# Last quarter of a second feed-forward product: two corrections on VectorE instead of accumulating DMA, and another place for the end of two row tiles

## The chip, the cores and the metric

The kernel runs on one core of a Trainium2 chip. A core has TensorE (PE, matrix products into PSUM), VectorE (DVE), ScalarE (ACT) and GpSimd (POOL), which run their own instruction streams and meet at semaphores, and SyncE (SP), which here only issues transfers. Transfers are issued from the SP, ACT and POOL queues and carried by 16 DMA engines. A transfer issued from POOL can add to what stands at its destination; the text calls that a *send*.

The metric is device time in microseconds (us) of one execution; each figure for a kernel is the median of its runs.

## The reference, cut to what matters

One encoder layer on 512 rows of width 1024. Attention branches give `h`; the part that matters here is the feed-forward block and the last norm, with `D_FF` = 4096:

```python
u2 = rmsnorm(h, g_ffn[l])
h = h + jnp.square(jax.nn.relu(u2 @ w_ff1[l])) @ w_ff2[l]
...
return rmsnorm(h, g_final)
```

`rmsnorm(h, g)` is `h * rsqrt(mean(h * h) + 1e-6) * g` by row.

## The kernel before

`h` lives in SBUF as four row tiles `hN[0..3]` of 128 x 1024 in float32 (the order listings call them `h_3650` to `h_3653`, the profile `h`). Every float32 product is made from two parts of each factor, a rounded `hi` (a cast on ACT, L203) and a remainder `lo` (a subtraction on DVE, L204), in three matmuls (`mm3`, L151 to L153: hi times hi, lo times hi, hi times lo). A weight therefore has to be loaded, cast and split before PE can use it.

The feed-forward block is done in four quarters of `D_FF` (`q` = 0 to 3). Within a quarter each of the two products is a 2 x 2 block product made of seven half-size products instead of eight, by Strassen's scheme in Winograd's form. The text calls the seven products of the second one P1 to P7. Their order is

```python
ORDER = (1, 2, 5, 6, 3, 7, 4)
```

`second_product(q)` runs over that list. For each product `n` it takes two weight chunks (`factor`, i = 0, 1), and for each of two row tiles `t` of 128 rows it accumulates 2 x 2 x 3 matmuls of 128 x 512, 24 in a product. Then `evac(q, n, t, ps)` adds the result to the quarter blocks of `h`: `C(i, j, t)` is column half `j` of row tile `2 * i + t`. So row tiles 0 and 1 are the upper row blocks, 2 and 3 the lower. Weights of P5, P6, P7 and P4 are sums of two chunks and are made by a send into the buffers `b11`, `b12` (`b` in the profile).

P1 and P5 stay in PSUM over all four quarters (`held`). P6 and P7 of the first three quarters are summed in `R6`, `R7`. In the last quarter (`last`) the pieces are put together:

- P1, P2: a copy from PSUM to a scratch tile `sq` on ACT, and a send of it into `C(0, 0, t)`. P1 also gives `R6[t] = P1 - R6[t]`.
- P6: E = `R6[t]` - P6, G = P5 - E (in `s1[t]`, the listing's `s_4588`, `s_4589`), both on DVE; then sends of E into `C(1, 0, t)` and of G into `C(1, 1, t)` and `C(0, 1, t)`.
- P3: a copy and a send into `C(0, 1, t)`.
- P7: two DVE adds into `C(1, 1, t)` and `C(1, 0, t)`.
- P4: a DVE add into `C(1, 0, t)`.

`C(0, 0, t)` is complete after P2, `C(0, 1, t)` after P6 and P3, `C(1, 1, t)` after P7 and `C(1, 0, t)` after P4.

`finish(t, c, n)` is the last norm of row tile `t`, in two calls. Each squares and sums column half `c` (`sumsq`, ACT, L805; with `n` = 0 a one-column step on DVE, L807, follows). With `n` = 0, or if `t < 2`, it multiplies the half by the gain `gl` (L1036), on POOL for row tiles 0 and 1 and on DVE for 2 and 3. With `n` = 1 it makes r (`ms` on DVE, L812; a power on POOL, L813), multiplies both halves by r (ACT, L1041, or r and gain in one DVE instruction, L1043) and writes them out (L1044), one from ACT's queue and one from SP's.

PE's order is that of the code. On the other engines a scheduler with its own model of time decides where an instruction stands in the stream, and each engine then takes its stream strictly in that order.

Of the kernel before, what the change touches and what calls it, by code (L numbers as in the profile page):

```python
# [14 lines left out]
ALU = mybir.AluOpType  # L15
# [46 lines left out]
def hybrid_block(ctx, tc, chunks, wst, xT, memT, xN, cols, gffn, gfin, wup, cst, out):  # L62
    nc = tc.nc
# [5 lines left out]
    def nm(s):  # L69
        uid[0] += 1  # L70
        return f"{s}_{uid[0]}"
# [13 lines left out]
    def at_(shape=None):  # L85
        return pa.tile(shape or [P, 512], F32, tag="a", name=nm("a"))
# [68 lines left out]
    def gT(key, rhi, rlo, evac, n=S):  # L155

        hi, lo = (t.rearrange("p (k c) -> p k c", k=KT) for t in (get_w(key) if isinstance(key[0], str) else key))
        ps = mmt()
        for k in range(KT):
            mm3(ps[:, :n], hi[:, k, :], lo[:, k, :], rhi[:, k, :], rlo[:, k, :], k == 0, k == KT - 1)  # L160
            if k == KT - 1:
                evac(ps)
            yield

    def gN(keys, lhs, nt, mk, evac, tail=1, get=None):


        pss = [mk() for _ in range(nt)]
        n = len(keys)
        steps = [[j] for j in range(n - tail)] + [list(range(n - tail, n))]  # L170
        for js in steps:
            ws = {j: [t.rearrange("p (k c) -> p k c", k=2) for t in (get or get_w)(keys[j])] for j in js}
            for t in range(nt):
                for j in js:
                    for kk in range(2):
                        k = 2 * j + kk
                        a, b = lhs(k, slice(t * P, (t + 1) * P))
                        mm3(pss[t], a, b, ws[j][0][:, kk, :], ws[j][1][:, kk, :], k == 0, k == 2 * n - 1)
                        if k == 2 * n - 1:
                            evac(t, pss[t])  # L180
                        yield
# [85 lines left out]
    with pool("front") as fp:  # L267
# [24 lines left out]
        ps = at_()  # L292
# [510 lines left out]
    def sumsq(sq, src, t, c, n):  # L803

        nc.scalar.activation(sq, src[:, 512 * c:512 * c + 512], AF.Square, accum_out=hss[:, t, n:n + 1])  # L805
        if n == 0:
            nc.vector.tensor_scalar(hss[:, t, 0:1], hss[:, t, 0:1], 1.0 / D, EPS, op0=ALU.mult, op1=ALU.add)  # L807

    def rms_tile(pool_, t):
        ms = pool_.tile([P, 1], F32, tag="ms", name=nm("ms"), bufs=2)  # L810
        r = pool_.tile([P, 1], F32, tag="rr", name=nm("rr"), bufs=2)
        nc.vector.tensor_scalar(ms, hss[:, t, 1:2], 1.0 / D, hss[:, t, 0:1], op0=ALU.mult, op1=ALU.add)  # L812
        nc.gpsimd.tensor_tensor(r, ms, mhalf[:, :1], op=ALU.pow)  # L813
        return r
# [81 lines left out]
    with pool("ff") as yp:  # L896
# [9 lines left out]
        def scratch():  # L906
            return yp.tile([P, S], F32, tag="sq", name=nm("sq"), bufs=2)

        def sub(to, x, y):
            nc.vector.tensor_tensor(to, x, y, op=ALU.subtract)  # L910

        def add(to, x, op=ALU.add):
            nc.vector.tensor_tensor(to, to, x, op=op)
# [115 lines left out]
        def finish(t, c, n):  # L1029

            sumsq(scratch(), hN[t], t, c, n)
            h = [hN[t][:, 512 * g:512 * g + 512] for g in range(2)]
            g_ = [gl[:, 512 * g:512 * g + 512] for g in range(2)]
            early = n == 0 or t < 2
            if early:
                (nc.gpsimd if t < 2 else nc.vector).tensor_tensor(h[c], h[c], g_[c], op=ALU.mult)  # L1036
            if n == 1:
                r = rms_tile(yp, t)
                for x in range(2):
                    if x != c or early:  # L1040
                        nc.scalar.mul(h[x], h[x], r)  # L1041
                    else:
                        nc.vector.scalar_tensor_tensor(h[x], h[x], r, g_[x], op0=ALU.mult, op1=ALU.mult)  # L1043
                    (nc.scalar if x != c else nc.sync).dma_start(out[t * P:(t + 1) * P, 512 * x:512 * x + 512], h[x])  # L1044

        def C(i, j, t):
            return hN[2 * i + t][:, 512 * j:512 * j + 512]

        def send(to, x):
            nc.gpsimd.dma_start(to, x, accum_op=ALU.add)  # L1050

        def evac(q, n, t, ps):
            last = q == NQ - 1
            if n == 1 and last:
                x = scratch()
                nc.scalar.copy(x, ps)
                send(C(0, 0, t), x)
                sub(R6[t], x, R6[t])
            if n == 2:
                if last:  # L1060
                    x = scratch()
                    nc.scalar.copy(x, ps)
                    send(C(0, 0, t), x)
                else:
                    add(C(0, 0, t), ps)
            if n in (6, 7) and not last:
                R = (R6 if n == 6 else R7)[t]
                if q == 0:
                    nc.scalar.copy(R, ps)
                else:  # L1070
                    add(R, ps)
            if n == 6 and last:
                E, G = R6[t], s1[t]
                sub(E, E, ps)
                sub(G, held[5][t], E)
                for to, x in ((C(1, 0, t), E), (C(1, 1, t), G), (C(0, 1, t), G)):
                    send(to, x)
            if n == 3:
                if last:
                    x = scratch()  # L1080
                    nc.scalar.copy(x, ps)
                    send(C(0, 1, t), x)
                else:
                    add(C(0, 1, t), ps)
            if n == 7 and last:
                add(C(1, 1, t), ps, ALU.subtract)
                finish(2 + t, 1, 0)
                add(C(1, 0, t), ps)
                finish(t, 0, 0)
                finish(t, 1, 1)  # L1090
            if n == 4:
                add(C(1, 0, t), ps)
                if last:
                    finish(2 + t, 0, 1)
# [152 lines left out]
```

## Time and profile before

| | us |
|---|---|
| median of three runs | 866.18 |
| lowest, highest | 865.49, 867.07 |
| span of the profiled execution, first to last instruction | 862.5 |

The page gives the profiled execution's span and not its own total; the median of the runs lies 3.7 us above that span. The mean granted TensorE clock of the core is 0.990.

How to read the lines: a busy time is the sum of the durations of an engine's instructions, and DMA issues, branches and semaphore steps are not counted. In a chain of waits each piece follows from what released it, and "issue" is time for which the profile shows no cause. In a timeline, the bracket behind an instruction is the engine's idle time before it and what ended it. The costliest groups of the page are the casts, splits and matmuls of the whole program:

```
L143 DVE TENSOR_TENSOR wlo<-raw,whi 128x1024 fp32r<-128x1024 f32 x80 | 101.7, 1275 | 104.1 <-ACT whi L142 103.5
L142 ACT CAST whi<-raw 128x1024 fp32r<-128x1024 f32 x80 | 84.1, 1053 | 132.3 <-PE mm L152 100.3
L151 PE MATMUL mm<-uhi,whi 128*128 128x512 f32 x360 | 142.5, 396 | 0.0
```

The last quarter of the second product runs from about 805 us to 849 us of the span, and the last norm and the writes of the output end it.

### The profile page before, as it was taken

The numbers are of one execution on the slowest core, as the hardware profiler recorded it, in microseconds if no ns is written. First come the engines' busy times: TensorE is split into PE (matmuls) and PEld (weight loads), VectorE is DVE, ScalarE is ACT, GpSimd is POOL, SyncE is SP. The second block draws the span as 40 slices with busy tenths as digits, with TensorE's granted clock in tenths as the row PEclk, the third lists the DMA queues.
The fourth block names the chain that finished last, engine by engine and source line by source line (L and its number), as shares of the span: only waits on it lengthen the run. The fifth ranks groups of instructions, "written<-read, shape, count | busy, mean of one in ns | idle before, by whom it ended". The sixth has DMA issues, their size and how long they took to land.

```text
span 862.5 us, 11811 instructions
## 1 busy us (share of the span) xinstructions
PE 839.0 (97%) x4513; PEld 711.2 (82%) x4513; DVE 542.4 (63%) x850; ACT 440.3 (51%) x703; POOL 113.0 (13%) x130
## 2 busy tenths in 40 slices
PE   8999999999999999999999999999999999999993
PEld 6778788888888888787888889888997899799872
DVE  5784656756444546474533547675688678778954
ACT  7764746754333432321332436565676377457744
POOL 5100000000000021221112100111001000100234
PEclk9999999999999999999999999999999999999997
DMA  8444745544547355336222413758757956785694
GB/s 320 145 150 168 201 135 178 146 171 123 171 133 230 125 150 168 97 113 231 98 98 98 170 50 118 225 124 204 243 171 162 265 199 171 179 256 176 138 170 133
DMA packets 37513, 142.37 MB, mean 165 GB/s; under 512 B 4592, under 2 KB 5392, under 8 KB 35728
## 3 DMA queue, kind: packets, MB, share of 16 engines
q1 hardware_dynamic: 27216, 93.36, 30.5%
q0 software_dynamic: 8448, 45.09, 24.8%
q10 hardware_dynamic: 1792, 3.16, 1.1%
q8 instruction: 35, 0.57, 0.3%
q14 instruction: 22, 0.18, 0.1%
HBM read 136.34 MB, written 27.28 MB: 190 GB/s over the span
## 4 chain that ended last, share of the span: by engine, by line
PE 74%; issue 12%; DMA 6%; DVE 3%; ACT 2%; POOL 1%; SPq 0%; POOLq 0%; ACTq 0%; DVEq 0%
PE mm L152 20%; PE mm L153 20%; PE mm L151 20%; DMA b<-in_wst_dram 6%; PE a L151 2%; PE a L152 2%; PE a L153 2%; ACT hi L203 1%; PE a L748 1%; DVE lo L204 1%; PE a L477 1%; DMA cst_s<-in_cst_dram 1%; PE a L765 1%; PE a L508 1%; PE a L507 1%
## 5 line engine op out<-in xcount | busy, mean ns | idle before, releaser
L143 DVE TENSOR_TENSOR wlo<-raw,whi 128x1024 fp32r<-128x1024 f32 x80 | 101.7, 1275 | 104.1 <-ACT whi L142 103.5
L142 ACT CAST whi<-raw 128x1024 fp32r<-128x1024 f32 x80 | 84.1, 1053 | 132.3 <-PE mm L152 100.3
L151 PE MATMUL mm<-uhi,whi 128*128 128x512 f32 x360 | 142.5, 396 | 0.0
L152 PE MATMUL mm<-ulo,whi 128*128 128x512 f32 x360 | 140.7, 391 | 1.4 <-DVE ulo L204 1.4
L153 PE MATMUL mm<-uhi,wlo 128*128 128x512 f32 x360 | 140.5, 390 | 0.0
L203 ACT CAST hi<-raw 128x1024 fp32r<-128x1024 f32 x58 | 60.5, 1048 | 44.7 <-PE mm L152 31.7
L204 DVE TENSOR_TENSOR lo<-raw,hi 128x1024 fp32r<-128x1024 f32 x58 | 70.6, 1222 | 17.6 <-ACT hi L203 17.6
L152 PEld LDWEIGHTS mm<-ulo,whi 128*128 128x128 f32 x360 | 67.7, 188 | 15.8 <-DVE ulo L204 2.9
L153 PEld LDWEIGHTS mm<-uhi,wlo 128*128 128x128 f32 x360 | 67.6, 188 | 14.6 <-DVE wlo L143 0.4
L151 PEld LDWEIGHTS mm<-uhi,whi 128*128 128x128 f32 x360 | 67.7, 188 | 13.5 <-issue 0.7
L204 DVE TENSOR_TENSOR lo<-b,hi 128x1024 fp32r<-128x1024 f32 x40 | 48.9, 1223 | 38.3 <-ACT hi L203 38.2
L203 ACT CAST hi<-b 128x1024 fp32r<-128x1024 f32 x40 | 41.9, 1048 | 57.5 <-PE mm L153 24.1
L152 PE MATMUL mm<-lo,ch 128*128 128x512 f32 x160 | 63.4, 396 | 2.5 <-DVE lo L204 2.5
L151 PE MATMUL mm<-hi,ch 128*128 128x512 f32 x160 | 63.1, 395 | 0.9 <-ACT hi L203 0.8
L153 PE MATMUL mm<-hi,cl 128*128 128x512 f32 x160 | 63.0, 394 | 0.0
L1050 POOL DMA_DIRECT2D b<-in_wst_dram x32 | 27.7, 865 | 267.1 <-DVE lo L204 210.2
L152 PE MATMUL mm<-u2l,hi 128*128 128x256 f32 x192 | 54.3, 283 | 0.0
L153 PE MATMUL mm<-u2h,lo 128*128 128x256 f32 x192 | 54.3, 283 | 0.0
L151 PE MATMUL mm<-u2h,hi 128*128 128x256 f32 x192 | 54.3, 283 | 0.0
L151 PE MATMUL mm<-u2sh,hi 128*128 128x256 f32 x144 | 40.8, 283 | 0.0
L152 PE MATMUL mm<-u2sl,hi 128*128 128x256 f32 x144 | 40.8, 283 | 0.0
L153 PE MATMUL mm<-u2sh,lo 128*128 128x256 f32 x144 | 40.8, 283 | 0.0
(349 smaller groups left out, 1945.5 us busy)
## 6 DMA issues: line engine op xcount, KB each, us to landing
raw<-in_wst_dram SPq DMA_DIRECT2D x122, 512.0 KB, 4.0
b<-in_wst_dram POOLq DMA_DIRECT2D x32, 512.0 KB, 5.3
T<-in_wst_dram POOLq DMA_DIRECT2D x12, 1024.0 KB, 8.4
raw<-T SPq DMA_DIRECT2D x24, 512.0 KB, 4.5
b<-in_wst_dram SPq DMA_DIRECT2D x16, 512.0 KB, 5.1
xr<-in_xT_dram SPq DMA_DIRECT2D x4, 512.0 KB, 8.1
nFb<-dF ACTq DMA_DIRECT2D x8, 256.0 KB, 3.8
h<-in_xN_dram SPq DMA_DIRECT2D x4, 512.0 KB, 7.6
```

The source lines that it names most:

```text
L142: cast = nc.scalar.copy(hi, raw)
L143: nc.vector.tensor_tensor(lo, raw, f(hi), op=ALU.subtract)
L151: nc.tensor.matmul(ps, lh, rh, start=start, stop=False)
L152: nc.tensor.matmul(ps, lh, rl, start=False, stop=False)
L153: nc.tensor.matmul(ps, ll, rh, start=False, stop=stop)
L203: nc.scalar.copy(hi, src)
L204: return nc.vector.tensor_tensor(lo, src, f(hi), op=ALU.subtract).ins
L477: nc.tensor.matmul(ps[:, :w], q, K[e][:, 1, :w], start=False, stop=True)
L507: nc.tensor.matmul(po[:, q0:], vv, PTh[:, c0:c0 + w], start=n == 0, stop=False)
L508: nc.tensor.matmul(po[:, q0:], vv, PTl[:, c0:c0 + w], start=False, stop=n == 3)
L748: nc.tensor.matmul(ps[:, t, :], kk[:, sl], qq[:, sl], start=True, stop=True)
L1050: nc.gpsimd.dma_start(to, x, accum_op=ALU.add)
```

## The change

```diff
-            early = n == 0 or t < 2
+            early = n == 0
             if early:
-                (nc.gpsimd if t < 2 else nc.vector).tensor_tensor(h[c], h[c], g_[c], op=ALU.mult)
+                nc.vector.tensor_tensor(h[c], h[c], g_[c], op=ALU.mult)
...
                 sub(G, held[5][t], E)
-                for to, x in ((C(1, 0, t), E), (C(1, 1, t), G), (C(0, 1, t), G)):
+                for to, x in ((C(1, 1, t), G), (C(1, 0, t), E)):
                     send(to, x)
+                add(C(0, 1, t), G)
+                finish(t, 0, 0)
             if n == 3:
+                add(C(0, 1, t), ps)
                 if last:
-                    x = scratch()
-                    nc.scalar.copy(x, ps)
-                    send(C(0, 1, t), x)
-                else:
-                    add(C(0, 1, t), ps)
+                    finish(t, 1, 1)
             if n == 7 and last:
                 add(C(1, 1, t), ps, ALU.subtract)
                 finish(2 + t, 1, 0)
                 add(C(1, 0, t), ps)
-                finish(t, 0, 0)
-                finish(t, 1, 1)
```

Three things happen. The two corrections of `C(0, 1, t)`, G and P3, are added by DVE and no longer copied and sent. `finish` of row tiles 0 and 1 is called at P6 (first half) and P3 (second half), where it was called at P7. And all products with the gain are on DVE; for row tiles 0 and 1 the second half is now multiplied by r and gain in one instruction, as for 2 and 3.

PE's stream is the same, and up to the last split of P5's weights so are all others. On DVE, this is the end of the stream before, from the first add of P7 on (`mm_7387`, `mm_7388` are P7, `mm_7465`, `mm_7466` P4; `x2` is two of a kind in a row):

```order
L913 TENSOR_TENSOR h_3652<-h_3652,mm_7387 128x512 x2
L913 TENSOR_TENSOR h_3653<-h_3653,mm_7388 128x512 x2
L807 TENSOR_SCALAR hss_3654<-hss_3654 128x1
L1036 TENSOR_TENSOR h_3652<-h_3652,gl 128x512
L807 TENSOR_SCALAR hss_3654<-hss_3654 128x1
L913 TENSOR_TENSOR h_3652<-h_3652,mm_7465 128x512
L807 TENSOR_SCALAR hss_3654<-hss_3654 128x1
L812 TENSOR_SCALAR ms_7430<-hss_3654 128x1
L1036 TENSOR_TENSOR h_3653<-h_3653,gl 128x512
L807 TENSOR_SCALAR hss_3654<-hss_3654 128x1
L812 TENSOR_SCALAR ms_7457<-hss_3654 128x1
L913 TENSOR_TENSOR h_3653<-h_3653,mm_7466 128x512
```

And this is the same stretch of the changed kernel's DVE stream, from behind the last split of a weight (P7 is `mm_7411`, `mm_7412`, P4 `mm_7459`, `mm_7460`):

```order
L1043 SCALAR_TENSOR_TENSOR h_3650<-h_3650,rr_7387,gl 128x512
L913 TENSOR_TENSOR h_3652<-h_3652,mm_7411 128x512 x2
L1043 SCALAR_TENSOR_TENSOR h_3651<-h_3651,rr_7404,gl 128x512
L913 TENSOR_TENSOR h_3653<-h_3653,mm_7412 128x512 x2
L807 TENSOR_SCALAR hss_3654<-hss_3654 128x1
L1036 TENSOR_TENSOR h_3652<-h_3652,gl 128x512
L913 TENSOR_TENSOR h_3652<-h_3652,mm_7459 128x512
L807 TENSOR_SCALAR hss_3654<-hss_3654 128x1
L1036 TENSOR_TENSOR h_3653<-h_3653,gl 128x512
L913 TENSOR_TENSOR h_3653<-h_3653,mm_7460 128x512
L812 TENSOR_SCALAR ms_7486<-hss_3654 128x1
L812 TENSOR_SCALAR ms_7509<-hss_3654 128x1
```

The two products by r of row tiles 0 and 1 now stand among P7's adds, and their ms steps have left this stretch; behind the last add stand only the two ms of row tiles 2 and 3, and their products.

On POOL, the end of the stream, with what goes (-) and what comes (+); the sends into `h_3650` and `h_3651` are those of G and P3:

```order
 L1050 DMA h_3652<-s_4588 128x512
-L1050 DMA h_3650<-s_4588 128x512
 L1050 DMA h_3653<-s_4589 128x512
-L1050 DMA h_3651<-s_4589 128x512
-L1050 DMA h_3650<-sq_7375 128x512
-L1050 DMA h_3651<-sq_7384 128x512
-L1036 TENSOR_TENSOR h_3650<-h_3650,gl 128x512 x2
-L1036 TENSOR_TENSOR h_3651<-h_3651,gl 128x512
-L813 TENSOR_TENSOR rr_7431<-ms_7430,cst_s 128x1
```

Four sends and the four products are gone; the four small powers (L813) stay, two of them before P7's end now.

On ACT, the changed stream around P6, with the semaphores that each instruction waits for (DMASW7 and DMASW1 are the sends of P2 into row tiles 0 and 1, DMASW0 the send that completes P6's second weight):

```order
L805 ACTIVATE sq_7332,hss_3654<-h_3650 128x512 [waits DMASW7_49,Activation_49]
L203 CAST hi_7317<-b_4099 128x1024 [waits DMASW0_49,PE_49]
L203 CAST ch_4591<-od_4587 128x512 [waits PE_49]
L805 ACTIVATE sq_7347,hss_3654<-h_3651 128x512 [waits DMASW1_49,Activation_49]
L203 CAST hi_7355<-raw_7353 128x1024 [waits DMAHW3_49,DVE_49,PE_49]
L203 CAST hi_7373<-raw_7371 128x1024 [waits DMAHW4_49,DVE_49,PE_49]
```

The two Squares (L805) are new here; the casts `hi_7355` and `hi_7373` behind them are P3's two weights. Before, these four casts stood in the same order with no Square among them.

## The prediction

> **What bounds the kernel now.** I read the page first, then the busy time by stage over the last stretch, then the chain of waits, then single engines. The page gives the span and says that TensorE is nearly always at work.
>
> ```profile
> span 862.5 us, 11811 instructions
> PE 839.0 (97%) x4513; PEld 711.2 (82%) x4513; DVE 542.4 (63%) x850; ACT 440.3 (51%) x703; POOL 113.0 (13%) x130
> ```
>
> PE is idle for 862.5 - 839.0 = 23.5 us in all, and the stage table shows where more than half of that lies (columns: stretch; its length; PE, PEld, DVE, ACT, POOL busy with counts; granted clock; DMA share; GB/s).
>
> ```profile
> 844.00:849.00 5.00, 4.87 (x22) 3.70 (x20) 3.21 (x10) 3.05 (x9) 1.68 (x3) 1.00 0.30 52
> 849.00:853.00 4.00, 0.00 (x0) 0.00 (x0) 2.64 (x5) 2.23 (x8) 4.00 (x4) 0.92 0.01 2
> 857.00:860.00 3.00, 0.00 (x0) 0.00 (x0) 0.00 (x0) 0.00 (x0) 0.00 (x0) 0.50 0.94 356
> ```
>
> From 849 on PE has nothing left, while POOL is busy for all of 849 to 853. The last matmul is this one:
>
> ```profile
> 848.48 0.39 PE L153 MATMUL mm<-hi,cl 128*128 128x512 f32 x1
> ```
>
> So the products end at 848.48 + 0.39 = 848.87, and 862.5 - 848.9 = 13.6 us follow without one. The chain of waits (start, length, what) says who fills them:
>
> ```profile
> 844.16 3.28 issue
> 847.48 1.81 POOL h L1036 x2
> ...
> 849.97 1.71 POOL h L1036
> 851.68 0.53 POOL rr L813
> ...
> 853.48 0.71 ACT sq L805 x2
> ...
> 854.55 0.90 issue
> ...
> 856.07 0.75 DVE h L1043
> ```
>
> The end is set by rows 0 and 1, whose last corrections come by accumulating DMA. Their four products with the gain run on POOL from 847.48; the r of rows 2 and 3 (L813) stands behind them on POOL, and the last Square (853.48) behind rows 0 and 1 on ACT. The last product with r ends at 856.07 + 0.75 = 856.82. The 3.28 us of "issue" are the last send on its way:
>
> ```profile
> 843.30 0.86 POOL L1050 DMA_DIRECT2D h<-sq  x1 [1.92 <-issue]
> h<-sq POOLq DMA_DIRECT2D x1, 256.0 KB, 3.3
> ```
>
> Issued at 843.30 it lands 3.3 us later, at 846.6, though its matmuls (P3) were done about 8 us before.
>
> **The change, first what leaves the end.** Four sends into rows 0 and 1 (two of G, two of P3), four POOL products, and the Squares, r and writes of rows 0 and 1 leave the stretch after 846; they move to P6, P3 and P7. What stays behind the last matmul is row tile 3: add P4, Square, ms, r, product, write. The same sequence stands undisturbed in the output projection, so I take its price from there:
>
> ```profile
> 504.51 0.69 DVE L832 TENSOR_TENSOR h<-h,mm 128x512 f32<-128x512 f32 x1 [2.92 <-PE mm L153]
> 506.05 0.21 DVE L812 TENSOR_SCALAR ms<-hss 128x1 f32<-128x1 f32 x1 [0.85 <-ACT hsq L805]
> 506.41 0.56 POOL L813 TENSOR_TENSOR rr<-ms,cst_s 128x1 f32<-128x1 f32 x1 [25.87 <-DVE ms L812]
> 507.00 1.42 DVE L839 SCALAR_TENSOR_TENSOR un<-h,rr,gf 128x512 f32<-128x512 f32 x2 [0.74 <-POOL rr L813]
> ```
>
> From the add's start to the product's start are 507.00 - 504.51 = 2.49 us. Placed at 848.87 + 0.05 (a handoff, estimated) = 848.92, the last product starts at 851.41 and ends 0.75 later (the L1043 row) at 852.16, where before it ended at 856.82: **4.66 us earlier**.
>
> **Is DVE free for it?** DVE gets more to do just there. Between the last split and the last add it now runs, in the order shown with the change, two products by r, four adds, two one-column steps (L807), two products with the gain and one more add. Its durations:
>
> ```profile
> 842.97 2.47 DVE L913 TENSOR_TENSOR h<-h,mm 128x512 f32<-128x512 f32 x4
> 845.42 0.68 DVE L1036 TENSOR_TENSOR h<-h,gl 128x512 f32<-128x512 f32 x1
> 848.85 1.71 DVE L1036 TENSOR_TENSOR h<-h,gl 128x512 f32<-128x512 f32 x1
> 852.18 1.25 POOL L1036 TENSOR_TENSOR h<-h,gl 128x512 f32<-128x512 f32 x1
> ```
>
> Four adds in 2.47 give a pace of (2.47 - 0.68) / 3 = 0.60 each. Seven such instructions, two products by r at 0.75 - 0.08 = 0.67 and two one-column steps at 0.07 make 4.20 + 1.34 + 0.14 = 5.68 us, so DVE is ready for the last add at 842.97 + 5.68 = 848.65, and 0.27 us are spare. This holds only if a product with the gain takes 0.68. The row of 1.71 is the one that ran while POOL multiplied too (POOL: 1.25 alone, and 1.71 for the one at 849.97 in the chain). With POOL's products gone I take 0.68; were both at 1.71, the last add would come 2 x 1.03 - 0.27 = 1.8 us late.
>
> [...]
>
> The same rows speak against one new neighbour. Row tile 2's product by r now starts on DVE right after row tile 3's ms, while POOL wants to begin row tile 3's r. If one waits for the other, as the pair at 849 did, r starts after the 0.75 us product: the last product then ends about 0.6 us later, at 852.75. No row shows this very pair, so it costs between 0 and 0.6; I take the 0.6, since the only pair of two-input operations on record did wait.
>
> **The writes.** They have a queue of their own:
>
> ```profile
> 852.99 0.38 ACTq L1044 DMA_DIRECT2D out_dram<-h  x1
> 853.00:854.00 1.00, 0.00 (x0) 0.00 (x0) 0.00 (x0) 1.00 (x3) 1.00 (x3) 0.50 0.11 45
> ...
> 859.00:860.00 1.00, 0.00 (x0) 0.00 (x0) 0.00 (x0) 0.00 (x0) 0.00 (x0) 0.50 0.84 313
> 860.00:861.00 1.00, 0.00 (x0) 0.00 (x0) 0.00 (x0) 0.00 (x0) 0.00 (x0) 0.50 0.00 0
> ```
>
> The first write, issued at 852.99, moves from about 853.9 (share 0.11 in that slice): 0.9 us. Bytes stop at about 859.85, 3.0 us after the last product, and the span ends 2.6 us after that. Eight writes of 256 KB crowd there now; four will, as rows 0 and 1 go out around 844. At 356 to 385 GB/s one takes some 0.7 us. Row tile 2's two, issued at about 851.3, move from 852.2 to 853.5. Row tile 3's two, issued at 852.75, move from 853.65 to 855.0; at 852.16 they would queue behind the others and be through at 854.9. Then 2.6 us: the span ends at 857.6 or 857.5. I take 857.5, **5.0 us less**. If the writes gain nothing over before (5.68 us from last product to end), it is 858.4, a gain of 4.1; if each engine handoff and the writes go a little better, 856.7, a gain of 5.8.
>
> **Ahead of the end.** The matmuls keep their order. New on DVE between P5 and P7 are four adds or products of 0.68 before P3's end, and two more behind it; on ACT two Squares at P6 and two behind P3 take the place of two copies. Cover:
>
> ```profile
> 832.00:838.00 6.00, 6.00 (x28) 4.95 (x27) 4.25 (x5) 2.69 (x3) 5.13 (x6) 1.00 0.95 166
> 838.00:844.00 6.00, 6.00 (x28) 4.95 (x28) 3.40 (x4) 2.58 (x3) 1.55 (x2) 1.00 1.02 173
> 836.38 1.23 DVE L204 TENSOR_TENSOR lo<-b,hi 128x1024 fp32r<-128x1024 f32 x1 [0.81 <-ACT hi L203]
> DMA to landing us min/median/max: 4.3/5.7/7.0
> ```
>
> DVE is idle for 1.75 and 2.6 us there, ACT for more than 3 in each; so splits move by under half a microsecond. The tightest is that of P7's second weight, done at 836.38 + 1.23 = 837.61. P7 and P4 are 48 matmuls at 0.23 that end at 848.87, so P7 begins at 837.9 and needs that weight halfway, at 840.6: 3 us in hand. The sends of G into row tiles 2 and 3 take at most 7.0 us (last row, the four h<-s): from about 836 they land by 843, and row tile 3 is not needed before 845. Cost: nothing; without the cover, up to 0.7 us per instruction. The one place with a new wait on a transfer comes next, as the first rival.
>
> **Rivals.** *Slower: ACT stuck on a send.* On ACT the Square of row tile 1 now waits for that tile's P2 send, and the casts of P3's two weights stand behind it.
>
> ```profile
> 818.88 0.95 POOL L1050 DMA_DIRECT2D h<-sq  x1
> h<-sq POOLq DMA_DIRECT2D x1, 256.0 KB, 8.1
> 825.79 1.05 ACT L203 CAST hi<-b 128x1024 fp32r<-128x1024 f32 x1 [3.24 <-DMA b<-in_wst_dram]
> 827.27 1.99 ACT L203 CAST hi<-raw 128x1024 fp32r<-128x1024 f32 x2
> 832.36 0.39 PE L151 MATMUL mm<-hi,ch 128*128 128x512 f32 x1
> 832.59 0.40 PE L152 MATMUL mm<-lo,ch 128*128 128x512 f32 x1
> ```
>
> It lands at 818.88 + 8.1 = 827.0. Square (0.7), cast (1.05) and split (1.25) take 3.0 us more, and P3's first matmul with lo starts at 832.59, so up to a landing at 829.5 PE feels nothing: 2.5 us in hand. Row tile 0's Square fits into the 3.24 us that ACT waits ahead of 825.79. Past 829.5 every microsecond is one on PE, with a slow clock on top:
>
> ```profile
> 829.00:830.00 1.00, 1.00 (x4) 0.80 (x3) 1.00 (x2) 0.26 (x1) 0.26 (x1) 0.50 0.24 25
> 832.00:833.00 1.00, 1.00 (x6) 0.82 (x5) 0.44 (x1) 0.44 (x1) 0.72 (x1) 1.00 1.00 201
> ```
>
> After the stalls on P6's weights the clock is 0.50 (four matmuls a microsecond against six); nine matmuls at twice 0.23 cost some 1.8 us. To eat 5.0 us the landing would have to come after 829.5 + 5.0 - 1.8 = 832.7, 13.8 us after issue. At 15 us the time is about 867.5. For it: a blocking place that was not there. Against: 8.1 is the longest send near. **0.03**.
>
> [...]
>
> *DVE becomes the bound.* If each of the eleven instructions costs 0.15 more (handoffs, a wait on r), the last add comes 1.65 - 0.27 = 1.4 us late, with some more at the r: a gain of 3.0, 863.2. For: only 0.27 us spare. Against: most inputs are long ready. **0.13**.
>
> *A better end.* The slow stretch after 827 also goes: 5.0 + 1.8, about 859.4. The wait that precedes it, on P6's weights, is untouched, so **0.08**.
>
> *It does not do what it says.* Rows 0 and 1 still end last, or a second slow stretch and DVE together eat the gain: within 1.7 us of before, about 865.5. The order shows the sends gone, so **0.05**.
>
> **How the numbers follow.** The profile's page gives no total for its execution; the median of the three runs, 866.18, is 3.7 above its span, and I let that stand: 866.18 - 5.0 = **861.2**. The forecast (gain 4.1 to 5.8) has 0.71. The range 859.5 to 863.3 takes in its bounds, the DVE rival and nearly the better end, with the runs' own spread of 1.6. 0.2% (1.7 us) is about what a measurement of this kernel can tell from no change. Faster: 0.71 + 0.13 + 0.08 = 0.92; same 0.05; slower 0.03.
>
> **What would show it.** Right: no L1036 on POOL, the last matmul still near 848.9, the last add within 0.3 us of it, the last product ending at 852 to 853, four writes after 850. The pair is decided by whether the last L813 lasts or waits some 0.6 us more beside L1043. Wrong: the last add well behind the last matmul (DVE), ACT idle on a DMA near 827 with PE stalled at 832 (the send), or a second stretch at clock 0.50.

## The result and the profile after

| | before | after |
|---|---|---|
| median (us) | 865.84 (863.35 to 868.94, 6 runs) | 860.09 (857.45 to 862.33, 6 runs) |
| span of the profiled execution | 862.5 | 857.9 |
| total of the profiled execution | not given | 859.66 |
| end of the last matmul | 848.87 | 848.93 |
| from there to the span's end (the *tail*) | 13.63 | 8.97 |

The changed kernel is faster: ratio 0.9938, 95% interval 0.9917 to 0.9959. That is 5.4 us of 865.84, with 3.6 to 7.2 inside the interval. In the two profiled executions PE finishes at the same moment, and all of the 4.6 us between the spans lies behind it. (That PE ends alike is a coincidence of these two executions; the part on the half clock below takes it apart.) One execution of the changed kernel with the gain on POOL took 1041.66 us at a granted clock of 0.749; it is left out of that kernel's ratio below, and its median of 861.42 would be 861.31 without it.

The page of the changed kernel:

```profile
span 857.9 us, 11799 instructions
PE 838.7 (98%) x4513; PEld 711.3 (83%) x4513; DVE 545.9 (64%) x858; ACT 438.7 (51%) x699; POOL 105.4 (12%) x122
```

Its stage table over the end (columns as before: stretch, length, PE, PEld, DVE, ACT, POOL with counts, granted clock, DMA share, GB/s):

```profile
844.00:849.00 5.00, 4.93 (x22) 3.75 (x20) 4.96 (x11) 2.55 (x7) 0.00 (x0) 1.00 0.55 210
849.00:853.00 4.00, 0.00 (x0) 0.00 (x0) 2.41 (x5) 2.23 (x5) 1.54 (x2) 0.93 0.24 93
```

Against before, POOL has nothing in 844 to 849 (before: 1.68) and 1.54 us in 849 to 853 (before: all 4.00). DVE has taken the work over: 4.96 of 5 us ahead of the last matmul's end, where it was 3.21. The last matmul, from PE's timeline:

```profile
848.54 0.39 PE L153 MATMUL mm<-hi,cl 128*128 128x512 f32 x1
```

The chain of waits of the changed kernel (start, length, what) no longer begins on a send:

```profile
848.71 0.24 PE mm L153
...
848.97 0.69 DVE h L913
849.66 0.14 DVE ms L812
...
849.86 0.55 POOL rr L813
850.41 0.35 issue
850.76 1.03 POOLq L1231
...
851.82 0.75 DVE h L1043
```

It runs from PE's last matmul through the last add, the two r on POOL and the last product. Before, its first pieces were 3.28 us behind the issue of the last send and 3.5 us of POOL products. The send itself lands at 846.59, and a Square on ACT (846.67 to 847.4) stands between it and the first POOL product.

### The profile page after: what moved, and what is told of

The parts are those of the page before. It is cut to its first block, busy times and chain, and to the rows that moved or that the text cites. A ratio compares the mean times of both kernels' runs of the same rounds, so it can differ in the third digit from the quotient of the medians.

```text
span 857.9 us, 11799 instructions
## 1 busy us (share of the span) xinstructions
PE 838.7 (98%) x4513; PEld 711.3 (83%) x4513; DVE 545.9 (64%) x858; ACT 438.7 (51%) x699; POOL 105.4 (12%) x122
## 4 chain that ended last, share of the span: by engine, by line
PE 74%; issue 11%; DMA 7%; DVE 3%; ACT 2%; SPq 0%; POOL 0%; POOLq 0%; ACTq 0%; DVEq 0%
PE mm L152 20%; PE mm L153 20%; PE mm L151 20%; DMA b<-in_wst_dram 7%; PE a L151 2%; PE a L152 2%; PE a L153 2%; DVE lo L204 1%; ACT hi L203 1%; PE a L748 1%; DMA cst_s<-in_cst_dram 1%; PE a L477 1%; PE a L765 1%; PE a L508 1%; PE a L507 1%
```

## Experiments

All of them are timed against the kernel before on the same chip. "Tail" is the span less the end of the last matmul, and "idle at P6" the sum of PE's waits between 815 and 835 us. "Last 113" is the time that the last 113 of PE's 4513 matmuls take, counted in the trace: they begin in P5, at 818 to 821 us, ahead of P6's waits. "Half clock" says whether the profiled execution shows PE at a granted clock of 0.50 near 828 to 834 us.

| kernel | median | before | ratio, 95% interval | tail | idle at P6 | last 113 | half clock |
|---|---|---|---|---|---|---|---|
| changed kernel, first | 860.09 | 865.84 | 0.9938, 0.9917 to 0.9959 | 8.97 | 1.91 | 28.62 | no |
| the adds only | 861.20 | 864.63 | 0.9960, 0.9948 to 0.9973 | 11.35 | 1.79 | 28.54 | no |
| the gain on DVE only | 863.35 | 864.63 | 0.9989, 0.9978 to 0.9999 | 11.56 | 2.24 | 30.51 | yes |
| both, finish late | 860.54 | 864.63 | 0.9952, 0.9937 to 0.9967 | 9.75 | 2.04 | 28.75 | no |
| changed, gain on POOL | 861.42 | 864.63 | 0.9969, 0.9951 to 0.9986 | 9.24 | 2.04 | 30.29 | yes |
| changed kernel again | 858.72 | 865.29 | 0.9928, 0.9915 to 0.9941 | 8.98 | 2.02 | 28.64 | no |
| changed, row tile 2 on ACT | 858.43 | 865.29 | 0.9927, 0.9911 to 0.9942 | 8.78 | 1.76 | 28.44 | no |
| changed, P2 by DVE | 856.62 | 865.29 | 0.9897, 0.9883 to 0.9910 | 8.83 | 0.78 | 27.16 | no |
| both of these | 856.56 | 864.76 | 0.9901, 0.9868 to 0.9934 | 8.64 | 0.92 | 27.35 | no |
| and P1 by DVE | 858.08 | 864.76 | 0.9917, 0.9887 to 0.9947 | 8.70 | 1.77 | 28.44 | no |

The kernel before has 30.28 us in the last 113 and a tail of 13.63 in its first profile. The sum of the two columns puts the nine kernels of the table in the order of their ratios, except that the adds alone and the gain on POOL change places and that P2 by DVE has the same sum with row tile 2 and without.

### One part at a time

The adds alone: G and P3 are added by DVE, while the last norm of rows 0 and 1 stays at P7 with its products on POOL.

```diff
-                for to, x in ((C(1, 0, t), E), (C(1, 1, t), G), (C(0, 1, t), G)):
+                for to, x in ((C(1, 1, t), G), (C(1, 0, t), E)):
                     send(to, x)
+                add(C(0, 1, t), G)
             if n == 3:
-                if last:
...
-                else:
-                    add(C(0, 1, t), ps)
+                add(C(0, 1, t), ps)
```

> Kernel before plus only the two corrections by DVE (sends of G and P3 into rows 0 and 1 gone; finish of rows 0 and 1 still called at P7, their gain products still on POOL). The tail meant is from the end of the last matmul to the end of the span: 13.6 us before, 9.0 after. Theory (late data and the queue behind it each hold the end): with the last correction in by 840 instead of 846.6, POOL's four products start near 845, when ACT has squared row tile 2 and row tile 0, instead of 847.5; they still take 5.2 us and r of rows 2 and 3 stands behind them: tail 11 to 12, gain 1.5 to 2.5 us. Rival (the sends are all that matters): tail 9 to 10, gain 4 to 5.

The tail is 11.35, so half of what the change takes from the end is there already. The median falls by 3.4 us, more than the 1.5 to 2.5 that were expected; in this kernel's profile the stretch at half clock is missing too, of which more below. What holds the rest is POOL. Its timeline in this kernel (start, length, engine, line, operation, tiles, and in the bracket the idle time before it and what ended it):

```profile
842.59 4.68 POOL L1036 TENSOR_TENSOR h<-h,gl 128x512 f32<-128x512 f32 x3 [8.16 <-ACT sq L805]
...
847.77 1.26 POOL L1036 TENSOR_TENSOR h<-h,gl 128x512 f32<-128x512 f32 x1
849.00 1.06 POOL L813 TENSOR_TENSOR rr<-ms,cst_s 128x1 f32<-128x1 f32 x2
851.08 0.55 POOL L813 TENSOR_TENSOR rr<-ms,cst_s 128x1 f32<-128x1 f32 x1 [1.02 <-ACT h L1041]
```

Without a send to wait for, the products start at 842.59 and not at 847.48, but four of them still take POOL to 849.0, and the r of three row tiles stand behind them.

The gain alone: the sends stay, and all products with the gain are on DVE.

```diff
-            early = n == 0 or t < 2
+            early = n == 0
-                (nc.gpsimd if t < 2 else nc.vector).tensor_tensor(h[c], h[c], g_[c], op=ALU.mult)
+                nc.vector.tensor_tensor(h[c], h[c], g_[c], op=ALU.mult)
```

> Kernel before plus only the gain products on DVE (all sends stay, finish of rows 0 and 1 still at P7). Theory: the last send still lands at about 846.6, the Squares of row tile 1 follow at 849, but no product waits on POOL any more: tail 10.5 to 11.5, gain 2 to 3 us. Rival (late data alone sets the end): tail 13 or more, gain under 1. Other rival (POOL's products are all that matters): tail 9 to 9.5, gain 4 to 5.

The tail is 11.56 where at most 11.5 was expected, and the time gained is 0.1%, less than the tail would give. The chain of waits of this kernel says what stays:

```profile
843.75 3.29 DMA h<-sq
...
847.13 0.12 ACT sq L805
...
851.55 0.56 POOL rr L813
...
853.00 0.38 ACT sq L805
```

It begins on the send of P3, as before the change; ACT's Squares, POOL's r and the last Square (853.00) queue behind it. So sends and POOL's products each hold the end, nearly one behind the other: taking the sends away shortens the tail by 2.28 us, the products by 2.07, and both (the next kernel) by 3.88, not much under the sum of 4.35. With the new place it is 4.66.

### The place alone

Both parts, but `finish` of rows 0 and 1 called at P7, as before the change.

```diff
                 add(C(0, 1, t), G)
-                finish(t, 0, 0)
             if n == 3:
                 add(C(0, 1, t), ps)
-                if last:
-                    finish(t, 1, 1)
...
                 add(C(1, 0, t), ps)
+                finish(t, 0, 0)
+                finish(t, 1, 1)
```

> Changed kernel with finish of rows 0 and 1 called at P7 again (sends gone, products on DVE, place undone). Theory: data are there by 840, but ACT has eight Squares behind P7 and DVE's last add stands behind the ms and products of rows 0 and 1: tail 10 to 11, that is 1 to 2 us longer than the changed kernel's 9.0. Rival (the place is worth nothing once the sends and POOL are out): tail 9.0 to 9.4.

The tail is 9.75, between the two expectations: the place is worth 0.8 us. The DVE timeline shows by which instruction:

```profile
847.72 0.75 DVE L1043 SCALAR_TENSOR_TENSOR h<-h,rr,gl 128x512 f32<-128x512 f32 x1
848.38 0.33 DVE L812 TENSOR_SCALAR ms<-hss 128x1 f32<-128x1 f32 x2
848.62 0.68 DVE L913 TENSOR_TENSOR h<-h,mm 128x512 f32<-128x512 f32 x1
```

PE ends at 847.85 here (its last matmul starts at 847.46 and takes 0.39). The last add stands behind a product by r and two ms of other row tiles and starts 0.77 us after that; in the changed kernel it starts 0.04 us after (848.97 against 848.93). That is the prediction's rival in which DVE becomes the bound, made to happen. The time, by the ratios 1.2 to 2.1 us above the changed kernel's, is not clearly told apart from it: the intervals overlap.

### Back to POOL

The changed kernel, with the products of rows 0 and 1 on POOL again (`early` for `t < 2`, and the engine chosen by row tile as before).

```diff
-            early = n == 0
+            early = n == 0 or t < 2
-                nc.vector.tensor_tensor(h[c], h[c], g_[c], op=ALU.mult)
+                (nc.gpsimd if t < 2 else nc.vector).tensor_tensor(h[c], h[c], g_[c], op=ALU.mult)
```

> Changed kernel with the gain products of rows 0 and 1 on POOL again (sends gone, finish at P6 and P3). Theory: the products now run near 826 to 832 and 840 to 843, far from the end, and DVE has four instructions less: tail 8.7 to 9.5, the same time as the changed kernel within 1 us. Rival (POOL's products cost wherever they stand, since they slow DVE's two-input instructions beside them or hold up the sends of weights behind them): 1 to 3 us slower than the changed kernel, with PE stalls at P7 or P4.

The tail, 9.24, is as expected: at this place POOL's products are long over when PE ends. The time is not within 1 us of the changed kernel: 861.42 lies 1.3 and 2.7 us above its two medians, each of them taken beside other runs of before (the interval of the ratio overlaps with the first of the two and not with the second). Two things in the profile can make it so. One of DVE's splits is longer beside POOL's work (0.72 us more than the row of 1.23 quoted in the prediction), with POOL's last product going on to 843.83 and two r following from 843.79:

```profile
842.96 1.95 DVE L204 TENSOR_TENSOR lo<-b,hi 128x1024 fp32r<-128x1024 f32 x1 [1.29 <-ACT hi L203]
```

And its profile has the stretch at half clock that the last experiment is about. PE does not wait for the lengthened split: behind P6 it has no wait at all. Its last 113 matmuls take 30.29 us, 1.66 more than the changed kernel's and as long as before's, which have the same stretch. So in this execution the stretch is all that PE loses, and the rival's stalls at P7 or P4 are not there. That it is the cause in the other runs too is not shown.

### The one place where the prediction put a wait

The prediction took 0.6 us for row tile 3's r on POOL standing beside row tile 2's product on DVE. In the changed kernel the pair is there. DVE's timeline, and then POOL's:

```profile
850.64 0.74 DVE L1043 SCALAR_TENSOR_TENSOR h<-h,rr,gl 128x512 f32<-128x512 f32 x1
```

```profile
849.86 0.55 POOL L813 TENSOR_TENSOR rr<-ms,cst_s 128x1 f32<-128x1 f32 x1 [6.16 <-DVE ms L812]
850.80 0.99 POOL L813 TENSOR_TENSOR rr<-ms,cst_s 128x1 f32<-128x1 f32 x1 [0.39 <-DVE ms L812]
```

The r that is alone takes 0.55 us, the one beside the product 0.99. To see whether the product is the cause, row tile 2 was made to multiply by the gain first, which moves its products by r to ACT:

```diff
-            early = n == 0
+            early = n == 0 or t == 2
```

> Changed kernel with row tile 2 multiplied by the gain first (DVE) and by r on ACT for both halves, so that no two-input DVE product stands beside row tile 3's r. Theory (DVE's product held POOL up): that r lasts 0.55 us again instead of 1.0, the last product starts 0.2 to 0.4 us earlier, tail 8.6 to 8.8; time equal within what can be measured. Rival (something else makes that r long, such as its place behind another r): it lasts 0.9 to 1.0 again and the tail is 9.0 or more.

```profile
849.51 1.06 POOL L813 TENSOR_TENSOR rr<-ms,cst_s 128x1 f32<-128x1 f32 x2 [6.76 <-ACT sq L805]
```

Two in 1.06 us: without the product on DVE the second r is as short as the first. The wait is shown, and it is 0.44 us. A second pair in the changed kernel agrees: another r, recorded from 842.27, takes 1.43 us beside a split of 1.23 on DVE (from 842.07), and in both pairs r ends 0.4 us after DVE's instruction. Taken away it brings little: the tail falls by 0.2 us (8.78 against 8.98), because the gain products now stand ahead of ms on DVE, and the time, 858.43 against 858.72, is not told apart.

### P6's weights

The changed kernel still has PE waiting for P6's weights. On POOL's queue the two sends of P2 stand between and right behind these weights, so P2 was also added by DVE, straight from PSUM:

```diff
-                if last:
-                    x = scratch()
-                    nc.scalar.copy(x, ps)
-                    send(C(0, 0, t), x)
-                else:
-                    add(C(0, 0, t), ps)
+                add(C(0, 0, t), ps)
```

> Changed kernel with P2's correction too added by DVE straight from PSUM (two ACT copies and two sends of 256 KB less, which stood on POOL among the sends that make P6's weights). Theory: P6's second weight then lands after 5.2 us instead of 7.5, PE's idle time at P6 (1.9 us in the changed kernel's trace) falls under 1.0, and the last matmul ends 0.7 to 1.5 us earlier; gain over the changed kernel 0.5 to 2 us. Rival (that weight waits for the chain of its own two sends, not for its neighbours): idle time at P6 stays at 1.5 to 2.2 us, same time.

PE's waits in the changed kernel:

```profile
825.28 0.50 PE L152 MATMUL mm<-lo,ch 128*128 128x512 f32 x1 [0.71 <-DVE lo L204]
828.52 0.50 PE L151 MATMUL mm<-hi,ch 128*128 128x512 f32 x1 [0.44 <-ACT hi L203]
829.78 0.50 PE L152 MATMUL mm<-lo,ch 128*128 128x512 f32 x1 [0.76 <-DVE lo L204]
```

and with P2 added by DVE:

```profile
822.42 0.50 PE L152 MATMUL mm<-lo,ch 128*128 128x512 f32 x1 [0.47 <-DVE lo L204]
825.76 0.50 PE L152 MATMUL mm<-lo,ch 128*128 128x512 f32 x1 [0.31 <-DVE lo L204]
```

1.91 us of waits become 0.78. The transfers that fill `b` (issued by POOL between 815 and 830 us, smallest, median and largest time to landing) say why; first the changed kernel, then this one:

```profile
DMA to landing us min/median/max: 5.4/5.6/7.5
```

```profile
DMA to landing us min/median/max: 5.1/5.1/5.5
```

The longest, P6's second weight (issued at 819.80 and at 817.80), lands 2.0 us sooner after its issue once P2's sends are gone. The median is 856.62, 2.1 us under the changed kernel on the same chip, and the intervals of the two ratios lie apart: it beats both kernels.

Two kernels go on from there. With row tile 2 on ACT as well:

> The changed kernel with two edits at once: P2's correction added by DVE from PSUM (two copies and two sends less), and row tile 2's last norm with the gain applied ahead of r, so that its products by r run on ACT. The computation is the same. If the two act on different places (weights of P6 at 823; the last r on POOL at 850), their gains add: PE idle at P6 about 0.8 us in all, last product matmul at about 845, the last L813 lasts 0.55 us, a tail behind the last matmul of about 8.7 us, and a time of about 856.4 us. Rival: DVE, which gets both, is late at the end: last add over 0.3 us behind the last matmul, tail 9.2 us or more, 857 us.

The tail is 8.64, the smallest of all, and the waits at P6 are 0.92, as the first theory has it. The forecast of PE's end (845) was wrong, it is 846.56; that forecast came from an execution without a stretch at half clock in its first 20 us, and this one has it. The median, 856.56, is that of P2 alone: the smaller tail of 0.2 us is below what these runs can tell.

And with P1's correction added by DVE too (`send(C(0, 0, t), x)` becomes `add(C(0, 0, t), x)`):

> The same, and P1's correction is also added by DVE (from the scratch copy that stays for R6), so that none of the four sends of P1 and P2 is left. Same computation. Theory (POOL's queue of transfers makes P6's weights late): P6's second weight send lands earlier than 823, PE idle at P6 falls below 0.5 us, and the time is 0 to 1.5 us below the kernel with P2 alone. Rival: P1's sends have long landed when P6's weights are sent, so nothing is gained, and the two more adds on DVE at 805 to 810 delay the splits of P2's and P5's weights: the same time or up to 1 us longer.

The rival holds in the trace: the waits at P6 are back at 1.77, and the last 113 matmuls take 28.44 us against 27.35. The median, 858.08, is 1.5 us above the kernel without the two adds, but the two intervals overlap, so the times alone do not tell them apart. DVE's timeline in this kernel:

```profile
812.69 0.69 DVE L913 TENSOR_TENSOR h<-h,sq 128x512 f32<-128x512 f32 x1
...
813.89 0.68 DVE L913 TENSOR_TENSOR h<-h,sq 128x512 f32<-128x512 f32 x1
...
815.70 1.22 DVE L204 TENSOR_TENSOR lo<-b,hi 128x1024 fp32r<-128x1024 f32 x1
```

and the same split in the kernel without these two adds:

```profile
814.84 1.22 DVE L204 TENSOR_TENSOR lo<-b,hi 128x1024 fp32r<-128x1024 f32 x1
```

The two adds (L913, h<-h,sq) stand ahead of the split that frees the buffer `b`, on a DVE that has no gap between 811 and 825 us. P6's transfer waits for that split (it is issued at 817.21, 0.29 us behind the split's end, and at 816.36, 0.30 behind, without the two adds), and starts later by two adds, some 1.2 us; the 0.86 between the two rows is less because PE runs 0.35 us earlier in this execution. P6 did not wait for P1's sends: its second weight lands 5.7 us after its issue with them and 5.6 without. It comes later by two instructions on a full engine.

### The stretch at half clock

The gain by the medians (5.4 and 6.2 us by the two ratios) is larger than what the tails give (13.63 - 8.97 = 4.66). Before's profile had a stretch at half clock behind P6's waits, the changed kernel's first profile has none. Both kernels were therefore profiled twice more (the second profile of before gave one run of 865.27 us and a tail of 13.37, its third one of 864.64 and 13.63, the third of the changed kernel one of 860.75 and 8.98):

> The kernel before once more, for its trace. Theory: tail 13.6 us within 0.3; the stretch at half clock after the stalls on P6's weights may be there or not. Rival (the eight sends cause that stretch, and the change removed it): it is there again, and again missing in the changed kernel's second trace.

> The changed kernel once more, on one chip with the next three. Theory: the tail (end of the last matmul to end of span) is 9.0 us again within 0.3, and the last row's r (L813) again lasts about 1.0 us beside the product L1043 of the row tile before it, where it lasts 0.55 alone. The end of the last matmul moves by 1 to 3 us from execution to execution, with the slow stretch of the clock. Gain over before 4 to 6 us.

> The kernel before once more, for a third trace. If the stretch of half clock at about 828 to 834 us belongs to this kernel, it is there again, and the last matmul ends at 848.9 or later; if it falls at random, it may be gone, and the last matmul then ends 1 to 1.8 us sooner.

> The changed kernel once more, for a third trace. If the half clock at 828 to 834 us does not belong to this kernel, PE's granted clock stays at or near 1.00 there and the last matmul ends near 848; if it falls at random, it may show, with a last matmul 1 to 1.8 us later. The tail is 8.9 to 9.1 us either way.

The stage table of before's third profile:

```profile
829.00:830.00 1.00, 1.00 (x5) 0.79 (x4) 1.00 (x2) 0.65 (x1) 0.65 (x1) 0.65 0.02 4
830.00:831.00 1.00, 1.00 (x3) 0.79 (x3) 1.00 (x2) 0.00 (x0) 0.00 (x0) 0.50 0.57 82
831.00:832.00 1.00, 1.00 (x4) 0.73 (x3) 0.96 (x2) 0.00 (x0) 0.00 (x0) 0.50 0.94 176
832.00:833.00 1.00, 1.00 (x5) 0.79 (x4) 0.04 (x1) 0.04 (x1) 0.75 (x1) 0.64 1.10 217
```

and of the changed kernel's third:

```profile
831.00:832.00 1.00, 1.00 (x5) 0.82 (x6) 1.00 (x3) 1.00 (x2) 0.85 (x1) 1.00 0.31 57
832.00:833.00 1.00, 1.00 (x6) 0.84 (x5) 1.00 (x2) 0.63 (x1) 0.03 (x1) 1.00 0.60 74
833.00:834.00 1.00, 1.00 (x7) 0.81 (x6) 1.00 (x2) 0.26 (x1) 0.00 (x0) 1.00 0.72 98
```

Three profiles of three show it before the change and none of three after, with waits at P6 of 2.01 to 2.27 us before and 1.91 to 2.02 after. PE is busy all through these stretches, so each costs about 1.7 us (3.4 us at half speed). The last 113 matmuls show it: 30.28, 30.32 and 30.51 us before, 28.62, 28.64 and 28.63 after, that is 1.6 to 1.9 us less in every pair. With the tail's 4.66 this makes about 6.3 us between the kernels from the 113th matmul before the end on, which lies inside the intervals of both gains.

That the profiled executions still end their matmuls alike (848.87, 850.13 and 849.27 before, 848.93, 847.92 and 850.02 after) comes from ahead of this stage, where the two programs are the same: those 113 matmuls begin at 818.59, 819.81 and 818.76 before and at 820.31, 819.28 and 821.39 after. One part of that is another stretch at half clock in the first 35 us, of 3.4, 3.4 and 6.8 us in before's profiles and 6.8 in each of the changed kernel's. What it costs can't be read from its length, because PE also waits there: 4.8 us in the first 36 us of before's first profile, 3.2 of them for DVE's splits.

Why the stretch at P6 comes or not is to be seen in the traces, as far as they go. In each of the 13 profiles that show more than one change of the granted clock, the changes lie whole multiples of 3.41 us apart (in before's first they come at 12.65, 16.06, 828.43, 831.85 and 852.33). This grid lies differently to the program from execution to execution: in before's three profiles the stretch at P6 begins 20.44, 19.47 and 19.97 us ahead of the end of the last matmul. Taking P6's waits by the steps of that grid, the step just ahead of each of the five stretches holds 1.53, 1.54 and 1.83 (before), 1.70 (gain on DVE) and 1.61 us (gain on POOL) of PE's waits. In the nine profiles without a stretch the fullest step holds 1.35 us or less. So in these profiles it is not the sum of the waits that tells the two cases apart, but how much of it falls into one step. In the changed kernel's first profile the second and third wait are only 1.20 us together. In its other two they are 1.57 and 1.49, against 1.52 to 1.84 before, and an edge of the grid cuts them: at 827.21 (seven steps ahead of a change of the clock at 851.10), within a wait from 826.77 to 827.58, and at 829.89 (seven steps ahead of one at 853.78), between the two. If the sum within a step decides, the missing stretch of the second profile at least is owed to where the grid fell, and not to the change; that is the author's inference from these profiles, and no run tests it. How often either kernel has it, three profiles don't say.

## Why the prediction was right, and where a size was off

861.2 was predicted, with a range of 859.5 to 863.3 and a gain of 5.0 us; 860.09 was measured, with a gain of 5.4 by the ratio. The mechanism held, but that 5.4 lies so near 5.0 is in part luck. The tail, which was to give all 5.0, gave 4.66, and the missing stretch at half clock, which was not in the sum, gave another 1.7 or so in the profiles. Point by point:

- **What leaves the end.** Right: the tail falls by 4.66 us, and no send or POOL product is left in it. The parts show that sends and POOL products each held the end (tails of 11.35 and 11.56 with one of them left), as the chain of waits had them one behind the other. One piece of that chain was misread: the 3.28 us of "issue" are not the last send alone, which lands at 846.59, 2.43 us into them; the other 0.85 is a Square on ACT.
- **The new end.** The last add was put at 848.92 and started at 848.97; the 0.05 for the handoff from PE, an estimate for which no row was given, measured 0.04 (848.97 against 848.93). The last product was to end at 852.75 and ended at 851.82 + 0.75 = 852.57. The 0.6 for the pair of r and product measured 0.44. The prediction says that no row shows this pair, but before's trace has it: row tile 2's product by r runs on DVE from 854.50 to 855.25, and row tile 3's r, whose ms ends at 854.50, starts at 855.49 and ends at 856.04. From the end of ms to the end of r that is 1.54 us, where the changed kernel's undisturbed r takes 0.62 and the one beside the product 1.07. This wait stands as 0.90 of "issue" in the chain that the prediction shows.
- **DVE.** Of the 0.27 us to spare for the last add 0.1 was left (the gain product ahead of it starts at 848.25, and DVE's pace is 0.60). But the stages ahead were fuller than their rows suggested. These had DVE idle for 1.75 and 2.6 us; now:

```profile
832.00:838.00 6.00, 6.00 (x28) 4.98 (x27) 6.00 (x10) 2.10 (x2) 3.50 (x4) 1.00 0.81 148
838.00:844.00 6.00, 6.00 (x28) 4.96 (x27) 5.63 (x9) 4.32 (x8) 1.97 (x2) 1.00 0.61 103
```

PE is busy for all of both, so the cover held. The late finish shows the rival at work with 0.77 us of lateness: an add behind other row tiles' work, and the tail longer by as much.
- **ACT stuck on a send.** It costs nothing, but it was near. ACT does wait 0.47 us for row tile 0's send (it lands at 824.87, the Square starts at 824.95), within a time in which it had nothing else to do. Row tile 1's send lands at 828.68, and its Square follows a cast without a wait 0.22 us later:

```profile
828.38 0.62 ACT L203 CAST ch<-od 128x512 fp32r<-128x512 f32 x1
828.90 0.63 ACT L805 ACTIVATE sq<-h 128x512 f32<-128x512 f32 x1
...
829.52 1.99 ACT L203 CAST hi<-raw 128x1024 fp32r<-128x1024 f32 x2
```

and PE has no wait behind 829.78.
- **The writes.** From the last product's end to the end of the span 4.75 us were forecast and 5.3 measured. The bytes stop about when forecast, and the quiet time behind them is 3.1 us where 2.6 were taken over from before:

```profile
853.00:854.00 1.00, 0.00 (x0) 0.00 (x0) 0.00 (x0) 0.00 (x0) 0.00 (x0) 0.50 0.97 369
854.00:855.00 1.00, 0.00 (x0) 0.00 (x0) 0.00 (x0) 0.00 (x0) 0.00 (x0) 0.50 0.82 316
855.00:856.00 1.00, 0.00 (x0) 0.00 (x0) 0.00 (x0) 0.00 (x0) 0.00 (x0) 0.50 0.00 0
```

This is the term that was too small, by 0.5 us; with the last product 0.18 earlier, the tail was 8.97 and not 857.5 - 848.87 = 8.63.
- **From span to time.** The 3.7 us between span and median were let stand. A profiled execution's total lies 1.8 us above its span (859.66 against 857.9), so before's own profile was of an execution of about 864.3, below the median. The difference of two spans was not hurt by it; the level was.
- **The better end.** Its condition, no half clock at P6, holds in the three profiles after, and its 859.4 lies between the medians 860.09 and 858.72. It had 0.08, on the argument that the wait ahead of it is untouched. The waits are nearly that (1.91 to 2.02 us, and 2.01 to 2.27 before), but the argument fails: with sums of 2.01 and 2.02 us the stretch comes in one profile, with 1.54 us of them in one step of the clock's grid, and stays away in another, with 1.13. Its price of 1.8 was given as nine matmuls at twice 0.23, which would be 2.07 more; measured over the last 113 matmuls it is 1.6 to 1.9.

## What to carry to other kernels

Price the new end of a kernel by the same sequence of instructions where it stands undisturbed elsewhere in the trace; here that gave the last add within 0.05 us, and the last product within 0.2 with 0.6 added for the new neighbour. A send that adds costs its landing time (3.3 to 8.1 us for the 256 KB sends of P2 and P3 before) and its place in the queue of transfers (P6's second weight landed after 7.5 us beside P2's sends and after 5.5 without them), and both can be somebody else's wait. An add on DVE was the better trade here where DVE had a gap (1.75 and 2.6 us idle in two stages before), and not ahead of a split that frees a weight buffer, where it had none (with P1's two adds the waits at P6 were 1.77 us, without them 0.92). Before a gain is put down to a place, look at several profiles of both kernels and compare the same instructions in each: a stretch at half clock where PE is busy is worth 1.7 us here, as much as many an edit, and the start of the program moves all that follows by up to 2.8 us (the last 113 matmuls begin at 818.59 to 821.39 in the six profiles of the two kernels).

## What was not expected of the hardware

- The stretches at half clock ahead of the end have two lengths. Added up from the slices, those at P6 last 3.4 us in each of before's three profiles; those of the first 35 us last 3.4 or 6.8 us, and in one execution (P2 by DVE) there is none. At P6, 1.53 us or more of PE's waits within one 3.41 us step of the clock's grid was followed by a slow stretch each of five times, and 1.35 us or less in none of nine profiles; 2.02 us spread over three steps passed without one (changed kernel, second profile), and 2.01 us with 1.54 in one step did not (before, second). In the first 15 us of the program, where PE's work is sparser (0.34 to 1.00 us busy in each microsecond from 1 to 15 in before's first profile), the two cases are not in that order: about 1.16 us was followed by half clock in one execution (before, third), and 1.23 us or more was not in another (changed kernel, third).
- In the changed kernel's first profile one POOL instruction on a single column (0.55 us alone, from 849.86) takes 0.99 us beside a 128x512 product on DVE (from 850.80), and 1.43 beside a 128x1024 split (from 842.27).
- P6's second weight, a transfer of 512 KB, lands 2.0 us sooner (5.5 us after its issue with P2 by DVE, against 7.5 in the changed kernel) without two adding transfers of 256 KB beside it.
